# Bank-taking steps of the recurrent mixers issued in groups, and a planner estimate that charges for changes of operand form

## The chip, the cores and the metric

The kernel runs on one core of one Trainium2 chip. The metric is the device time of one execution in microseconds; three executions of the kernel before gave 1696.43, 1697.85 and 1698.03 us, median 1697.85.

## What is computed

Two layers of a hybrid encoder over 768 tokens (256 of a prompt, 512 of a sample; six tiles of 128 tokens). Each layer normalises, multiplies by one wide projection, runs three mixers side by side (windowed attention, a bidirectional mLSTM with 4 heads, a bidirectional Mamba-2 SSD with 8 heads), and merges them by gates and output projections:

```python
proj = rms_norm(x, norm_g) @ w_in
ya = window_attention(aq, ak, av, attn_sink) * silu(az)
yb = rms_norm(mlstm_bidir(mq, mk, mv, mi, mf)) * sigmoid(mo) * silu(mz)
yc = rms_norm(ssd_bidir(sx, sbm, scm, dt, a, d_skip) * silu(sz))
merged = ga * (ya @ w_att_out) + gb * (yb @ w_mlstm_out) + gc * (yc @ w_ssm_out)
return x + merged @ w_out
```

In the SSD each head needs, for each direction, a matrix of decays exp(acs_t - acs_s) under a causal mask; it is multiplied with C B^T and then with the head's inputs:

```python
lmat = exp(where(causal, acs[:, :, :, None] - acs[:, :, None, :], -inf))
y_diag = einsum('zclsg,zclsge,zcsgep->zclgep', cb, lmat, xdt)
```

## The kernel before, in words

**Products.** The large products (projection, gates, output projections) run on the TensorE in fp32r: every fp32 operand is split into a high and a low fp32r part, and three products are added. `mm_c` makes 128 output channels by all 768 tokens: for each of the three terms a matmul of 512 and one of 256 columns, here called a pair. A projection item has 24 pairs, an output product 12. `mm_t` makes a tile of 128 tokens by up to 512 channels. Weights come by DMA, are cast to the high part on ScalarE (`CAST R<-F`) and to the low part on VectorE (`TENSOR_TENSOR R<-F,R`), both in `split_w`. All small products of the mixers are plain fp32 (`psum<-F`): transposes, chunk states, scores and the products of the heads. So the TensorE changes between two forms of operand.

**The order of the work.** The whole program is written out in one pass by a planner; no engine reorders anything. The fp32r products form the backbone, in the order of the list `ORDER`. After every few matmuls `mm_c` and `mm_t` call `tick`, which lets waiting work go in between: tasks (`any_task`), weight splits (`split_next`) and mixers (`any_mixer`, two lanes). A mixer is a Python generator; it yields where it must wait, for a number of PSUM banks (`yield 1`, `yield 2`, `yield "pair"`), for an event, or for the time at which what it issued last is estimated to be done. `step` resumes it if `task.ready` has come by the planner's clock; where it wants banks, `grab` must find them free. The clock is an estimate: `Watched.cost` gives each instruction a length, and `Clock.note` adds it to the engine's time, behind what it depends on. `now` is the estimated time of the TensorE. `push` goes on without products where an item needs something that is not there yet.

**The mixers.** Lane 0 runs per layer: two attention groups (A0, A1), the four mLSTM heads (M), the SSD (S). `mix_ssd` first makes eight chunk states (`state`: GpSimd scales the inputs, two fp32 matmuls of 64 output rows, `64x256` in the order, then VectorE). Then six score products (`products`), then the heads (`head`, at most three at work). A head loads two broadcast rows of decays from HBM (`F<-csd`, 384 KB each, on SyncE's queue); for each direction VectorE subtracts and masks (six `SCALAR_TENSOR_TENSOR 128x128`), ScalarE takes the exponential (`ACTIVATE F<-F 128x768`) and, for the first direction, scales six times (`ACTIVATE 128x128`); VectorE adds the directions (six more) and multiplies with the scores (`TENSOR_TENSOR 128x768`); then come the head's six matmuls, `128x64`. Last, `across` adds what the chunk states give. `q_put` and `k_put` normalise and turn queries and keys at the start of a layer (GpSimd's power, then VectorE, for keys ScalarE, then transposes).

**Beside the heads** run the items `ob`: a gate product into PSUM, read by ScalarE (`ACTIVATE F<-psum 128x768`), an output product, read by VectorE (`SCALAR_TENSOR_TENSOR F<-F,psum`), an addition on GpSimd, and a store (`mg<-F`) on SyncE. Gate products take the two pairs of PSUM banks 0 to 3 in turn, so one waits for that reading ScalarE instruction.

Of the kernel before, what the change touches and what calls it, by code (L numbers as in the profile page):

```python
# [10 lines left out]
F32R = mybir.dt.float32r  # L11
# [15 lines left out]

RESERVE = 5000
AHEAD = 5
D = 1024  # L30
KD = 8
NT = 6
# [69 lines left out]
class Arena:  # L102
# [7 lines left out]
    def __init__(self, ap, words):  # L110
        self.ap, self.words = ap, words
        self.holes = [(0, words)]
# [200 lines left out]
class Watched:  # L313


    def __init__(self, engine, key, clock):
        self.engine, self.key, self.clock = engine, key, clock

    def __getattr__(self, name):
        fn = getattr(self.engine, name)  # L320
# [12 lines left out]
    def cost(self, name, out, ins, kw):  # L333
        n = 1
        for _, k in out.ap[1:]:
            n *= k
        key = self.key
        if key == "pe":
            if name == "transpose":
                return 107.0  # L340
            if ins[0].dtype == F32R:
                return 13.0 + n / 2.4

            if out.offset // out.ap[0][0] == 64:
                return 12.0
            return max(110.0 * 2, n / 0.6 + 6.0)
        if name == "dma_start":
            return 128 * n * 4 / 360.0
        if name == "tensor_reduce":
            n = 64 * n  # L350
        if key == "dve":
            three = name == "scalar_tensor_tensor" and all(a.tensor.name != self.clock.psum for a in ins)
            return 67.0 + n / 0.96 + (62.0 if three else 0.0)
        if key == "act":
            return 55.0 + 0.88 * n + (93.0 if "accum_out" in kw else 0.0)
        if kw.get("op") == ALU.pow:
            return 390.0 + 157.0 * n
        if name == "tensor_scalar":
            return 130.0 + 3.1 * n
        return 130.0 + 2.2 * n  # L360
# [47 lines left out]
class Body:  # L408
    def __init__(self, tc, es, ins, outs):
        self.tc = tc  # L410
        self.ins, self.outs = ins, outs
        self.clk = Clock()
        nc = self.nc = Watch(tc.nc, self.clk)
        sb = es.enter_context(tc.tile_pool(name="sb", bufs=1))
        ps = es.enter_context(tc.tile_pool(name="ps", bufs=1, space=bass.MemoryType.PSUM))
        dr = es.enter_context(tc.tile_pool(name="dr", bufs=1, space=bass.MemoryType.DRAM))
        RW, FW, WSLOT = 12288, 20096, 2048
        self.H = sb.tile([128, 2, KD, TOK], F32R, name="H")
        rt = sb.tile([128, RW + 4 * WSLOT], F32R, name="R")
        self.R = Arena(rt[:, 0:RW], RW)  # L420
        self.wslots = [rt[:, RW + WSLOT * j:RW + WSLOT * j + WSLOT] for j in range(4)]
        ft = sb.tile([128, FW], F32, name="F")
        self.F = Arena(ft, FW)
        self.psum = ps.tile([128, 8, 512], F32, name="psum")
        for t in (self.H[:, 0, 0, :], rt[:, 0:8], ft[:, 0:8]):
            self.clk.add(t)
        self.clk.add(self.psum[:, 0, :], True)
        self.held = [False] * 8
        self.x1 = dr.tile([TOK, D], F32, name="x1")
        self.mg = [dr.tile([8, 128, TOK], F32, name=f"mg{i}") for i in range(2 * NL)]  # L430
        self.tg = [dr.tile([8, 128, TOK], F32, name=f"tg{i}") for i in range(NL)]
        self.csd = [dr.tile([2, 48, 128], F32, name=f"csd{i}") for i in range(NL)]
        self.md = [dr.tile([2, 24, 128], F32, name=f"md{i}") for i in range(NL)]

        self.K = self.F.alloc(K_N).ap
        nc.sync.dma_start(out=self.K[:, K_ID:K_ID + 128], in_=ins["kst"][:, K_ID:K_ID + 128])
        self.ident = self.K[:, K_ID:K_ID + 128]
        self.masks = (self.K[:, K_MF:K_MF + 128], self.K[:, K_MB:K_MB + 128])
        self.expo = self.F.alloc(8).ap
        nc.vector.memset(self.expo, -0.5)  # L440
        self.raw_slots = [self.F.alloc(1024).ap for _ in range(2)]
        self.raw_extra = []
        self.cb = Ring(self.F, 1, CB_N)
        self.cc = Ring(self.F, 1, CC_N)
        self.zz = self.F.alloc(224).ap
        nc.vector.memset(self.zz, 0.0)
        self.ones = self.F.alloc(1).ap
        nc.vector.memset(self.ones, 1.0)

        self.pieces = []  # L450
        self.items = []
        self.wide, self.extra = set(), set()
        off = 0
        for l in range(NL):
            for kind, name, idx, pcs in item_plan(l):
                ids = []
                for p in pcs:
                    k, c = piece_shape(p)
                    ids.append(len(self.pieces))
                    self.pieces.append((off, k, c))  # L460
                    off += 128 * k * c
                self.items.append((l, kind, name, idx, ids))

                if kind == "W":
                    self.wide.update(ids)
                if name in ("akv", "sz"):
                    self.extra.update(ids)
        self.raw_of, self.w_of, self.w_task = {}, {}, {}
        self.n_raw = self.n_split = self.asked = 0
        self.raw_drop = []  # L470
        self.tasks = []
        self.done = {}
        self.lanes = [[], []]
        self.h_task, self.h_high = {}, [False] * NT
        self.S = [dict() for _ in range(NL)]


# [50 lines left out]
    def step(self, task, now):  # L528
# [11 lines left out]
        if isinstance(w, Room):  # L540
            if not w.there():
                return False
        elif isinstance(w, Task):
            if not w.over or w.ready > now:
                return False
        elif isinstance(w, tuple):
            if w not in self.done or self.done[w] > now:
                return False
        elif w is not None:
            got = self.grab(w, now)  # L550
            if got is None:
                return False
        kept, self.clk.last = self.clk.last, 0.0
        try:
            task.want = task.gen.send(got)
# [48 lines left out]

    def tick(self):

        while True:
            now = self.now
            if self.any_task(now) or self.split_next(now):
                continue  # L610
            if max(self.clk.free["dve"], self.clk.free["act"]) > now + BACKLOG or not self.any_mixer(now):
                return

    def push(self, until):

# [186 lines left out]
    def norm(self, x, g, i, sc, st):  # L802
# [3 lines left out]
        yield  # L806
        self.rstd(st[:, 1:2], st[:, 0:1], 1.0 / D)
        yield
# [19 lines left out]
    def layer0_start(self):  # L828
# [18 lines left out]
        for i in range(NT):  # L847
            self.h_task[i] = self.spawn(first(i, xr.next()))
            if i == 0:
                nc.sync.dma_start(out=gb.ap, in_=self.ins["ng"][0:1, :].to_broadcast([128, D]))  # L850
            if i < 2:
# [399 lines left out]
    def fetch(self, l, c):  # L1251

        s, nc = self.S[l], self.nc
        olds = s.setdefault("olds", {})
        for j in range(c, min(c + AHEAD, 8)):
            if j in olds:
# [664 lines left out]
```

## Time and profile before

| | us |
|---|---|
| median of three executions | 1697.85 |
| profiled execution, device time | 1698.3 |
| its span in the trace | 1696.5 |
| PE busy in the span | 1669.7 (98%) |
| DVE busy | 909.3 (54%) |
| ACT busy | 629.3 (37%) |
| POOL busy | 299.7 (18%) |
| granted TensorE clock, mean | 0.998 |

Times are counted from the start of the span. The TensorE is busy nearly throughout, so what counts is where it waits and how long its instructions hold it. Every instruction is recorded under one line (L323, a helper), so rows are told apart by engine, operands and shape. One fp32 matmul of the order stands in the trace as two records, unless it is a transpose. A row of the timeline merges instructions that follow each other on an engine: the start, the time they span, the count, and in brackets how long the engine sat idle before them and who ended that. The shape in a merged row is that of its first instruction. Ends of matmuls are modelled and reach some 0.2 us into the next row, so times of the TensorE are best read from start to start.

### The profile page before, as it was taken

What the parts mean: (1) busy time and instruction counts of PE and PEld (TensorE: products, weight loads), DVE (VectorE), ACT (ScalarE), POOL (GpSimd) and SP (SyncE); (2) the same over time, 40 slices, a digit from 0 to 9 for tenths busy, and PEclk for the clock granted to TensorE, in tenths of its full rate; (3) what the DMA queues carried; (4) which work ended last, traced back from release to release, by engine and by line L of the source; (5) the groups of instructions that cost most, each with busy time, mean ns of one, the idle gap of its engine ahead of it and who ended that gap; (6) DMA issues with size and microseconds to landing.
All of it is one profiled execution on the core that took longest, in us unless ns stands there. A gap on an engine that the chain in (4) does not pass through costs nothing.

```text
span 1696.5 us, 25376 instructions
## 1 busy us (share of the span) xinstructions
PE 1669.7 (98%) x9902; PEld 1435.2 (85%) x9902; DVE 909.3 (54%) x2112; ACT 629.3 (37%) x1377; POOL 299.7 (18%) x396
## 2 busy tenths in 40 slices
PE   7999999999999999999999999999999999999999
PEld 6888889888887888888878888898888878888887
DVE  6664446454485982246356544474455859723441
ACT  5446653232332532233224466442333344232320
POOL 4513210000002112014034132100000021301220
PEclk9999999999999999999999999999999999999999
DMA  5101122222213542245211101222121145331522
GB/s 203 63 27 38 51 76 78 87 69 64 68 63 114 190 147 91 72 144 175 78 44 63 52 26 50 88 88 78 69 72 60 63 140 174 134 109 44 174 87 75
DMA packets 47880, 152.17 MB, mean 90 GB/s; under 512 B 5616, under 2 KB 6544, under 8 KB 47760
## 3 DMA queue, kind: packets, MB, share of 16 engines
q1 hardware_dynamic: 47760, 150.55, 26.4%
q8 instruction: 78, 1.28, 0.3%
q14 instruction: 42, 0.34, 0.1%
HBM read 131.51 MB, written 19.02 MB: 89 GB/s over the span
## 4 chain that ended last, share of the span: by engine, by line
PE 87%; POOL 4%; DVE 3%; issue 3%; DMA 2%; ACT 1%; SPq 0%; POOLq 0%; ACTq 0%; DVEq 0%
PE psum L323 87%; POOL F L323 4%; DVE F L323 2%; DMA F<-csd 1%; DVE R L323 1%; DMA F<-wts_dram 1%; ACT F L323 0%; DMA F<-cstb_dram 0%; ACT R L323 0%; SPq L323 0%; ACT H L323 0%; DVE H L323 0%; POOLq L323 0%; ACTq L323 0%; DVEq L323 0%
## 5 line engine op out<-in xcount | busy, mean ns | idle before, releaser
L323 PE MATMUL psum<-H,R 128*128 128x512 f32 x4800 | 887.8, 341 | 0.0
L323 PEld LDWEIGHTS psum<-H,R 128*128 128x128 f32 x4800 | 734.1, 188 | 106.7 <-issue 6.5
L323 PE MATMUL psum<-R,H 128*128 128x512 f32 (+2 forms) x1752 | 386.2, 375 | 0.9 <-DVE F L323 0.5
L323 PEld LDWEIGHTS psum<-R,H 128*128 128x128 f32 x1752 | 306.1, 188 | 54.9 <-DVE R L323 1.4
L323 DVE TENSOR_TENSOR R<-F,R 128x1024 fp32r<-128x1024 f32 (+3 forms) x178 | 220.0, 1244 | 237.2 <-ACT R L323 235.2
L323 DVE SCALAR_TENSOR_TENSOR F<-F 128x128 f32<-128x128 f32 (+5 forms) x596 | 244.4, 456 | 76.8 <-POOL F L323 33.8
L323 POOL TENSOR_TENSOR F<-F 128x512 f32<-128x512 f32 (+9 forms) x216 | 203.3, 951 | 430.8 <-DVE F L323 255.0
L323 ACT ACTIVATE F<-F 128x128 f32<-128x128 f32 (+8 forms) x432 | 201.8, 496 | 207.2 <-DVE F L323 199.8
L323 PE MATMUL psum<-F 128*128 128x128 f32 (+5 forms) x2006 | 250.7, 288 | 22.6 <-DVE F L323 13.4
L323 PEld LDWEIGHTS psum<-F 128*128 128x128 f32 (+2 forms) x2006 | 203.0, 163 | 64.8 <-DVE F L323 22.0
L323 PE MATMUL psum<-R 128*128 128x512 f32 (+2 forms) x1344 | 250.1, 336 | 0.0
L323 ACT CAST R<-F 128x1024 fp32r<-128x1024 f32 (+3 forms) x226 | 195.1, 874 | 99.4 <-DVE F L323 58.3
L323 PEld LDWEIGHTS psum<-R 128*128 128x128 f32 x1344 | 204.4, 188 | 31.3 <-issue 3.6
L323 ACT ACTIVATE F<-psum 128x768 f32<-128x768 f32 (+2 forms) x124 | 89.0, 718 | 364.9 <-PE psum L323 329.9
L323 POOL TENSOR_SCALAR F<-F 128x256 f32<-128x256 f32 (+7 forms) x112 | 72.7, 652 | 755.0 <-ACT F L323 542.8
L323 ACT COPY F<-psum 128x256 f32<-128x256 f32 (+6 forms) x262 | 95.1, 400 | 176.6 <-PE psum L323 168.8
L323 DVE SCALAR_TENSOR_TENSOR F<-F,psum 128x768 f32<-128x768 f32 (+3 forms) x124 | 88.4, 725 | 102.8 <-ACT F L323 54.4
L323 DVE SCALAR_TENSOR_TENSOR F<-psum,F 128x128 f32<-128x128 f32 (+4 forms) x75 | 37.5, 505 | 172.8 <-PE psum L323 170.7
L323 DVE TENSOR_TENSOR F<-F 128x2 f32<-128x2 f32 (+8 forms) x316 | 86.3, 283 | 42.4 <-POOL F L323 22.7
L323 DVE TENSOR_SCALAR F<-F 128x128 f32<-128x128 f32 (+5 forms) x230 | 63.0, 302 | 41.0 <-ACT F L323 22.2
L323 DVE TENSOR_TENSOR F<-F,psum 128x129 f32<-128x129 f32 (+2 forms) x104 | 35.8, 376 | 36.4 <-ACT F L323 25.6
L323 DVE CUSTOM_DVE_ANT_0 F<-psum,F 128x256 f32<-128x256 f32 (+1 forms) x96 | 40.9, 464 | 10.4 <-PE psum L323 9.1
(24 smaller groups left out, 267.0 us busy)
## 6 DMA issues: line engine op xcount, KB each, us to landing
F<-wts_dram SPq DMA_DIRECT2D x164, 512.0 KB, 3.6
mg<-F SPq DMA_DIRECT2D x32, 384.0 KB, 2.9
F<-mg SPq DMA_DIRECT2D x32, 384.0 KB, 4.2
F<-csd SPq DMA_DIRECT2D x32, 384.0 KB, 7.0
F<-x_dram SPq DMA_DIRECT2D x12, 512.0 KB, 6.3
F<-md SPq DMA_DIRECT2D x16, 384.0 KB, 4.8
x<-F SPq DMA_DIRECT2D x6, 512.0 KB, 2.6
F<-x SPq DMA_DIRECT2D x6, 512.0 KB, 3.8
```

The lines of the kernel that those rows point to most:

```text
L323: r = fn(*args, **kw)
```

## The change

Two things are changed in the planner. No operand, tile or computation differs; only the order in which instructions stand does.

First, `Watched.cost` adds 50 ns to a TensorE instruction whose form (fp32r or not) differs from that of the one before.

Second, `tick` gets a gate. While the task at the head of lane 0 is an mLSTM head or the SSD (`calm`), steps that take PSUM banks may go in a tick only once the planner's clock has reached `gate`; a tick in which one went sets the gate 2000 ns ahead. Within an open tick any number may go. The gate holds for all tasks, not for lane 0 alone, and not in `push`.

```diff
+GROUP = 2000.0
...
         if key == "pe":
+            turn = 0.0 if self.split == (ins[0].dtype == F32R) else 50.0
+            self.split = ins[0].dtype == F32R
             if name == "transpose":
-                return 107.0
+                return 107.0 + turn
             if ins[0].dtype == F32R:
-                return 13.0 + n / 2.4
+                return 13.0 + n / 2.4 + turn
             if out.offset // out.ap[0][0] == 64:
                 return 12.0
-            return max(110.0 * 2, n / 0.6 + 6.0)
+            return max(110.0 * 2, n / 0.6 + 6.0) + turn
...
         elif w is not None:
+            if not self.open:
+                return False
             got = self.grab(w, now)
             if got is None:
                 return False
+            self.out = True
...
     def tick(self):
+        self.open, self.out = self.now >= self.gate or not self.calm(), False
         while True:
             now = self.now
             if self.any_task(now) or self.split_next(now):
                 continue
             if max(self.clk.free["dve"], self.clk.free["act"]) > now + BACKLOG or not self.any_mixer(now):
-                return
+                break
+        if self.out:
+            self.gate = self.now + GROUP
+        self.open = True
+
+    def calm(self):
+        return bool(self.lanes[0]) and self.lanes[0][0][0][1] in ("M", "S")
```

The order of the fp32r products is the same in both kernels; what stands between them moves. Stretches of fp32 matmuls on the TensorE go from 251 to 245; those of half-array matmuls (64 output rows, `64x...`) from 57 to 52.

**TensorE, the keys of layer 0.** The product of the last queries and the keys' projection (`128x288`); `F 128x128 x4` is the last query tile's transposes, each `F 128x128 x2` those of a key tile, in turn. Before:

```order
L323 MATMUL psum<-R,H 128x288 x60
L323 MATMUL psum<-F 128x128 x4
L323 MATMUL psum<-R,H 128x288 x6
L323 MATMUL psum<-F 128x128 x2
L323 MATMUL psum<-R,H 128x288 x18
L323 MATMUL psum<-F 128x128 x2
L323 MATMUL psum<-R,H 128x288 x24
```

and now:

```order
L325 MATMUL psum<-R,H 128x288 x54
L325 MATMUL psum<-F 128x128 x4
L325 MATMUL psum<-R,H 128x288 x30
L325 MATMUL psum<-F 128x128 x2
L325 MATMUL psum<-R,H 128x288 x12
L325 MATMUL psum<-F 128x128 x2
L325 MATMUL psum<-R,H 128x288 x12
```

The queries stand 6 products earlier, the first key tile 18 and the second 12 products later; the third stands where it did.

**SyncE's queue, the first heads of layer 0's SSD.** `F<-csd` are the heads' decays, `F<-mg` and `mg<-F` the load and store of an `ob` item, `F<-wts_dram` a piece of weights. Before:

```order
L323 DMA F<-wts_dram 128x1024
L323 DMA F<-mg_70 128x768
L323 DMA mg_71<-F 128x768
L323 DMA F<-csd_76 128x768 x6
L323 DMA F<-wts_dram 128x1024
```

and now:

```order
L325 DMA F<-wts_dram 128x1024
L325 DMA F<-mg_70 128x768
L325 DMA F<-csd_76 128x768 x6
L325 DMA mg_71<-F 128x768
L325 DMA F<-wts_dram 128x1024
```

The store has gone behind the six loads. The load of `mg` ahead of them now takes another buffer, and waits for the last of the score products.

**ScalarE, the same place.** From the copies of the score products on. `F<-F 128x768` is an exponential, `F<-F 128x128 x6` the scaling, `F<-psum` the reading of a gate product, `CAST` a weight split. Before:

```order
L323 COPY F<-psum 128x384 x4
L323 ACTIVATE F<-F 128x768
L323 ACTIVATE F<-F 128x128 x6
L323 ACTIVATE F<-psum 128x768
L323 CAST R<-F 128x1024
L323 ACTIVATE F<-F 128x768
L323 ACTIVATE F<-F 128x128 x6
L323 ACTIVATE F<-F 128x768
L323 CAST R<-F 128x1024
```

and now:

```order
L325 COPY F<-psum 128x384 x4
L325 ACTIVATE F<-F 128x768
L325 ACTIVATE F<-F 128x128 x6
L325 ACTIVATE F<-F 128x768
L325 ACTIVATE F<-F 128x128 x6
L325 ACTIVATE F<-psum 128x768
L325 CAST R<-F 128x1024
L325 ACTIVATE F<-F 128x768 x2
L325 CAST R<-F 128x1024
```

The exponential and the scalings of the second head have gone ahead of the reading of the gate product and of the cast. On the TensorE the score products stand 6 pairs earlier than before; the first three heads stand 14, 4 and 14 pairs earlier, the fourth 4, the other four as before. In layer 1 all of these stand at the same places.

## Rows read from the trace of the kernel before

**Rows 1.** TensorE's waits: total us, times, longest us.
```profile
PE psum L323 <- DVE F L323: 13.9, 12, 5.5
PE psum L323 <- ACT F L323: 6.2, 6, 1.2
```
**Rows 2.** Stages: us, busy by engine (count), clock, DMA share, GB/s; layer 0's mLSTM.
```profile
230.00:540.00 310.00, 310.00 (x1914) 271.59 (x1913) 176.21 (x397) 102.31 (x217) 21.30 (x27) 1.00 0.24 76
```
**Rows 3.** Timeline of TensorE, layer 0, the chunk states.
```profile
526.21 1.51 PE L323 MATMUL psum<-F 128*64 128x256 f32 x12
...
529.26 0.65 PE L323 MATMUL psum<-F 128*64 128x256 f32 x4
...
530.74 0.65 PE L323 MATMUL psum<-F 128*64 128x256 f32 x4
```
**Rows 4.** Timeline of TensorE, layer 0, score products and first three heads.
```profile
542.29 1.61 PE L323 MATMUL psum<-F 64*128 64x128 f32 x24
543.83 7.33 PE L323 MATMUL psum<-H,R 128*128 128x512 f32 x40
...
567.45 1.55 PE L323 MATMUL psum<-F 128*128 128x64 f32 x12 [1.45 <-DVE F L323]
...
570.02 1.55 PE L323 MATMUL psum<-F 128*128 128x64 f32 x12 [0.26 <-DVE F L323]
...
579.95 1.45 PE L323 MATMUL psum<-F 128*128 128x64 f32 x12
```
**Rows 5.** Timeline of SyncE's queue, the same place.
```profile
543.86 0.33 SPq L323 DMA_DIRECT2D mg<-F  x1
544.23 4.14 SPq L323 DMA_DIRECT2D F<-csd  x6
```
**Rows 6.** The chain that ended last, the third of these loads.
```profile
545.22 8.40 DMA F<-csd
```
**Rows 7.** Timeline of DVE, the same place.
```profile
549.30 1.66 DVE L323 SCALAR_TENSOR_TENSOR F<-F 128x128 f32<-128x128 f32 x6 [7.36 <-DMA F<-csd]
553.72 3.24 DVE L323 SCALAR_TENSOR_TENSOR F<-F 128x128 f32<-128x128 f32 x12 [2.75 <-DMA F<-csd]
556.88 1.21 DVE L323 TENSOR_TENSOR R<-F,R 128x1024 fp32r<-128x1024 f32 x1
...
561.16 0.94 DVE L323 SCALAR_TENSOR_TENSOR F<-F,psum 128x768 f32<-128x768 f32 x1
...
563.16 3.25 DVE L323 SCALAR_TENSOR_TENSOR F<-F 128x128 f32<-128x128 f32 x6
566.44 0.96 DVE L323 TENSOR_TENSOR F<-F 128x768 f32<-128x768 f32 x1
...
569.88 0.61 DVE L323 SCALAR_TENSOR_TENSOR F<-F,psum 128x384 f32<-128x384 f32 x1
```
**Rows 8.** Timeline of ACT, the same place.
```profile
551.00 2.74 ACT L323 ACTIVATE F<-F 128x768 f32<-128x768 f32 x7 [6.11 <-DVE F L323]
553.64 0.79 ACT L323 ACTIVATE F<-psum 128x768 f32<-128x768 f32 x1
554.34 1.03 ACT L323 CAST R<-F 128x1024 fp32r<-128x1024 f32 x1
```
**Rows 9.** Timeline of TensorE, layer 1, its first head.
```profile
1406.73 1.55 PE L323 MATMUL psum<-F 128*128 128x64 f32 x12 [1.25 <-DVE F L323]
```
**Rows 10.** Timeline of TensorE, key transposes: first and last of layer 0, fourth of layer 1.
```profile
68.91 0.44 PE L323 MATMUL psum<-F 128*128 128x128 f32 x2 [1.18 <-ACT F L323]
...
88.09 0.44 PE L323 MATMUL psum<-F 128*128 128x128 f32 x2 [0.99 <-ACT F L323]
...
917.52 0.44 PE L323 MATMUL psum<-F 128*128 128x128 f32 x2 [0.71 <-ACT F L323]
```
**Rows 11.** Timeline of TensorE, transposes in the first microseconds, after a wait.
```profile
15.03 1.97 PE L323 MATMUL psum<-F 128*128 128x128 f32 x8 [5.45 <-DVE F L323]
```
**Rows 12.** Stages, columns as in rows 2: around that wait.
```profile
11.20:18.00 6.80, 2.97 (x11) 2.77 (x12) 5.23 (x7) 4.67 (x8) 1.97 (x5) 0.50 0.94 369
```

More of the change, by code (lines that the diff above doesn't have):

```diff
@@ L317, in __init__ @@
         self.engine, self.key, self.clock = engine, key, clock
+        self.split = False
     def __getattr__(self, name):
@@ L474, in __init__ @@
         self.h_task, self.h_high = {}, [False] * NT
+        self.open, self.gate, self.out = True, 0.0, False
         self.S = [dict() for _ in range(NL)]
```

## The prediction

> **What bounds the kernel now.** First the busy times in the table: the TensorE (PE) works for 1669.7 of 1696.5 us, and since the change gives it the same instructions, only its waits, and what an instruction costs beside its neighbours, can move the time. So second the list of its waits: the two rows that matter are those for VectorE (12 waits) and ScalarE (6), 20.1 us together [rows 1]; 5.5 of it is one wait in the first microseconds, which the change doesn't touch. Third the stages: in the mLSTM of layer 0, where the gate acts most, the PE has no wait at all (310.00 busy of 310.00) [rows 2]. Fourth the timeline at each wait that is left: they lie at the norms, queries and keys at the start of a layer [rows 10], and before the first two heads of each layer's SSD [rows 4, 9]. At these the PE runs ahead of a chain of other engines. There the order decides, and I read what stands before and behind each wait in the orders shown above.
>
> **Fewer and longer stretches.** The orders have 251 stretches of fp32 work before and 245 after, so 12 changes of form fewer. No row prices one alone; 12 times the 0.05 us that the diff books is 0.6 us from above, zero from below; I take 0.1. More is saved where half-array matmuls join. One chunk state alone and two pairs of products fill 529.26 to 530.74, 1.48 us; three states joined and four pairs fill 526.21 to 529.26, 3.05 us [rows 3]. A pair costs (567.45 - 1.45 - 543.83) / 62 = 0.358 us (62 pairs lie between the score products and the first head) [rows 4]. So a state alone costs 0.76 us, three joined 1.62: each joining saves 0.33 us. Before, the states stand as 3, 1, 1, 1, 1, 1; now as 3, 2, 1, 2: two joinings, 0.66 us per layer. Attention has one stretch of half-array work fewer and `across` joins one more per layer; at 0.33 and half of that (not shown; zero to 0.33 each) another 0.6. Together 0.1 + 1.3 + 0.6 = 2.0 us gained, sure to within 0.8.
>
> **The first head of the SSD.** It now stands behind 54 pairs instead of 62, and the score products 6 pairs earlier. The PE's time first. Three states at 526.21; then 1.62, 6 pairs 2.15, two states 1.19 (midway between the two prices), 2.15, 0.76, 2.15, 1.19, 2.15: the score products start at 539.6 instead of 542.29 [rows 4] and end 1.54 later, at 541.1. After 54 pairs, 19.3 us, the PE would be at head 0 at 560.4. Before it was there at 566.0 and waited until 567.45 [rows 4].
>
> The data second. The six loads of decays were issued at 544.23, behind a store that had waited for GpSimd [rows 5]; this store now stands behind them, and a load that waits for the last score product stands ahead. So they go at 541.1 plus 0.55 for that load's issue (its like before took 0.33 to 0.55) = 541.65, 2.6 us earlier, not 5.6. Landing after issue as before: the first at 549.30 - 2.6 = 546.7 [rows 7], the third, which VectorE waits for next, 8.40 after its issue [rows 6]: 545.22 - 2.6 + 8.4 = 551.0. Sooner than the first's 5.1 us after issue it can't well be (547.8); an `mg` load and a piece of weights ahead could make it a microsecond later.
>
> From there ScalarE's new order counts. VectorE's six for the second head end at 552.7 (1.66 [rows 7]). ScalarE then takes the exponential and six scalings, 2.74, to 555.4, and only then reads the gate product, 0.79, and casts, 1.03 [rows 8]: 557.3. The weights' low part on VectorE waits for the cast: 1.21, 558.5. Behind it in order come six masks 1.66, the `ob` item's 0.94, the sum of the directions 3.25, the multiplication 0.96 [rows 7]: 565.3. So head 0 starts at 565.3 and the PE loses 4.9 us where it lost 1.45. Part of it comes earlier: the next gate product needs the bank that ScalarE reads until 556.2, and the PE is there after 39 pairs, at 555.0. That is 1.2 us of the 4.9, not more.
>
> **Heads 1 and 2.** Head 1 (12 pairs on, 4 earlier than before): VectorE needs a weight part 1.21, the first head's result 0.61 [rows 7] (from 566.9 on), 1.66 and 0.96: 570.1; the PE is there at 565.3 + 1.37 + 12 x 0.358 = 571.0. The 0.26 lost before [rows 4] goes. Head 2 (14 pairs on): masks 1.66, result 0.61 (from 572.5), weight part 1.21, sum 3.3, multiplication 0.96: 578.6; the PE is there at 571.0 + 1.37 + 5.0 = 577.4, and loses 1.2. Then level with before: 578.6 + 1.37 + 14 pairs 5.0 = 585.0, where before the head at 579.95 was done at 581.3 [rows 4]. So layer 0 loses 3.7 us here, the states' 0.66 and 2.77 us of moved work already in it. Bounds: with the third load at 547.8 the chain waits 2.1 less at best (ScalarE's scalings for the first head end at 551.2): 1.6 lost; with the loads 1 us later and head 3 late as well, 6. Layer 1 has the same orders at the same places, and its first head waits 1.25 [rows 9]: again 3.7. Sum 7.4, with the joining of states taken off.
>
> **Starts of the layers.** Here no gate holds; only the 50 ns move steps. Layer 0: the last queries go 6 products of 288 columns earlier, each 288 / 768 of a pair, 0.134 us; if their chain gives the time, 0.8 is lost, if not, nothing; I take 0.8. Keys 0 and 1 go 18 and 12 products later: their waits, 1.18 and nearly as much, go: 2.2 gained. The last key goes 2 pairs earlier onto a chain that is already late by 0.99 [rows 10]: 0.7 lost. Net 0.7 gained. Layer 1: the fourth key, 0.71 late already [rows 10], goes 6 products earlier, 0.8 lost, and the last 2 pairs earlier, 0.7 lost: 1.5. Both starts: 0.8 lost; -1 to +2.
>
> **The sum.** 7.4 + 0.8 - 0.7 (joinings outside the states) = 7.5; I round to 7.2, since a queue ahead of head 0 may hide some tenths. The mLSTM I cost at nothing: its steps now stand mostly 6 pairs, 2.1 us, apart, further from what they wait for, and the heads have no deadline near. Were that cover gone, a step's wait would be like those at the keys, 1 us. The profiled execution took 1698.3 us (span 1696.5), 0.45 above the median: 1698.3 + 7.2 = 1705.5, and beside the median 1705.0.
>
> **The clock.** After 5.45 us without work the PE's transposes took 1.97 us [rows 11], and from 11.20 to 18.00 the granted clock was 0.50, the lower of its two levels [rows 12]; it ran at full speed through waits of 1.5 us and less. From 15.03 to 18.00 at half speed costs 1.5 us. Head 0's wait of 3.7 us lies between. The Trainium skill (TensorE: Matmul & The Clock Gate, Part 1) says that an idle array falls to the lower clock and must work for a while before it gets the higher one back; that trace agrees. By that rule the two waits at head 0 would add up to 3.0 us.
>
> **The rivals.**
> A. The clock falls at head 0 of both layers, or head 3 waits too: 1705.0 + 3.0 = 1708. For it: the wait is over twice the longest that kept the clock. Against: part of it lies ahead, at the gate product, and a slower PE comes later to head 2, which takes back 1.2 per layer. Chance 0.2.
> B. No change. The chain to head 0 moves as far as the PE: the third load lands within 5.1 us, and the sum of directions takes 1.66, as where its instructions don't wait for each other, not 3.25. Then 1.6 less again per layer, so nothing is lost at the heads, and 1697.85 + 0.8 - 0.7 = 1698. Against: the loads of a burst landed one after another. Chance 0.15.
> C. Faster. The groups stand late enough: the heads' 1.7 and 1.5 us of waits go, the joinings give 2.0, keys 0 and 1 give 2.2: 1697.85 - 7.4 = 1690.5; with half the waits kept, 1693. For it: everywhere in the mLSTM and the states steps do stand later. Against: heads 0 and 2 stand earlier. Chance 0.12.
>
> **How the numbers follow.** My forecast has 0.53, at 1705.0, and its own range is 1701.5 to 1708.5. With B's upper and A's lower part, 8 in 10 lie in 1697 to 1710.5. A measurement of this kernel tells about 0.2%, 3.4 us, from no change. Slower by more: the forecast's 0.53 less 0.04, and A's 0.2, 0.69. Faster: C's 0.12. No change: 0.19.
>
> **What would show it.** Right: a wait for VectorE of some 4 us before each layer's first head, one of about 1 us for ScalarE at the gate product before it, the loads of decays issued 2 to 3 us earlier; two chunk states in about 1.2 us; waits gone at keys 0 and 1 of layer 0, grown at the last keys. Wrong: head 0 starting at once, loads issued before 541, a new wait in the mLSTM, or 1.66 us for the first sum of directions. The clock at 0.50 behind head 0 would show A.

## The result

The changed kernel takes 1712.84 us (median of four runs, 1712.34 to 1720.24); the kernel before, run beside it, 1697.94. The ratio is 1.010, with a 95% interval from 1.0083 to 1.0117: slower by 14.9 us. The forecast was 7.1 slower, its range ended at 1710.5. The side was right, the size was half.

TensorE's waits in the profile after (columns as in [rows 1]; the profiled execution took 1712.67 us, its span 1710.9):
```profile
PE psum L325 <- DVE F L325: 17.5, 14, 5.4
PE psum L325 <- ACT F L325: 11.8, 11, 2.4
...
PE psum L325 <- DVE R L325: 1.9, 2, 1.5
```
Against [rows 1], waits for VectorE grew by 3.6 us and those for ScalarE by 5.6; the last row was 0.4 before. That is 10.7 of the span's 14.4 us. The rest is no wait, as will be seen.

The place of the prediction, layer 0's SSD, on TensorE (columns of [rows 3, 4]):
```profile
529.47 1.52 PE L325 MATMUL psum<-F 128*64 128x256 f32 x12
...
542.78 1.61 PE L325 MATMUL psum<-F 64*128 64x128 f32 x24
...
560.38 7.38 PE L325 MATMUL psum<-H,R 128*128 128x512 f32 x32 [2.38 <-ACT F L325]
569.18 1.55 PE L325 MATMUL psum<-F 128*128 128x64 f32 x12 [1.42 <-DVE F L325]
570.54 4.59 PE L325 MATMUL psum<-H,R 128*128 128x512 f32 x16
...
576.36 1.45 PE L325 MATMUL psum<-F 128*128 128x64 f32 x12
...
582.64 1.45 PE L325 MATMUL psum<-F 128*128 128x64 f32 x12
...
595.35 8.59 PE L325 MATMUL psum<-H,R 128*128 128x512 f32 x48 [0.80 <-ACT F L325]
...
605.28 1.55 PE L325 MATMUL psum<-F 128*128 128x64 f32 x12 [0.66 <-DVE F L325]
```
The first states stood at 526.21 [rows 3]: 3.26 us are gone before the SSD begins. Then the gate product waits for ScalarE, head 0 for VectorE, heads 1 and 2 for nothing, and later a gate product and head 3 wait again. The row at 570.54 has 8 pairs in 4.59 us, without a wait in front.

Stages of the same trace around these waits (columns of [rows 2]):
```profile
560.60:564.00 3.40, 3.40 (x11) 2.89 (x11) 2.70 (x7) 3.08 (x4) 0.00 (x0) 0.51 0.14 30
564.00:569.10 5.10, 3.76 (x22) 3.06 (x20) 5.07 (x10) 2.72 (x7) 1.89 (x1) 1.00 0.44 163
570.80:574.20 3.40, 3.40 (x12) 2.82 (x12) 3.37 (x10) 0.00 (x0) 0.00 (x0) 0.50 0.85 211
```
The granted clock, third number from the end, was 0.50, the lower level, for 3.4 us right behind the gate product's wait, then full, then 0.50 again behind head 0's.

The other engines in the same microseconds (columns of [rows 5, 7, 8]). SyncE's queue, the loads of decays:
```profile
544.83 4.94 SPq L325 DMA_DIRECT2D F<-csd  x6
```
They are issued in one run, as in [rows 5], 0.6 us later by the clock and 2.7 earlier against the states. VectorE, from the first masks to head 0's multiplication:
```profile
551.74 1.67 DVE L325 SCALAR_TENSOR_TENSOR F<-F 128x128 f32<-128x128 f32 x6 [5.46 <-DMA F<-csd]
...
561.30 1.23 DVE L325 TENSOR_TENSOR R<-F,R 128x1024 fp32r<-128x1024 f32 x1 [1.61 <-ACT R L325]
...
564.01 0.95 DVE L325 SCALAR_TENSOR_TENSOR F<-F,psum 128x768 f32<-128x768 f32 x1
564.88 3.26 DVE L325 SCALAR_TENSOR_TENSOR F<-F 128x128 f32<-128x128 f32 x6
568.17 0.96 DVE L325 TENSOR_TENSOR F<-F 128x768 f32<-128x768 f32 x1
```
Its first load landed 6.9 us after the issue; the low part (561.30) waited for ScalarE. The third load, which the second head's masks wait for (columns of [rows 6]):
```profile
545.77 9.01 DMA F<-csd
```
ScalarE:
```profile
553.44 2.75 ACT L325 ACTIVATE F<-F 128x768 f32<-128x768 f32 x7 [8.07 <-DVE F L325]
556.90 2.74 ACT L325 ACTIVATE F<-F 128x768 f32<-128x768 f32 x7 [0.71 <-issue]
559.54 0.79 ACT L325 ACTIVATE F<-psum 128x768 f32<-128x768 f32 x1
560.23 1.03 ACT L325 CAST R<-F 128x1024 fp32r<-128x1024 f32 x1
```
The second row of seven is the second head's; it stood behind the gate product's read in [rows 8] and now stands ahead of it. GpSimd:
```profile
565.04 1.89 POOL L325 TENSOR_TENSOR F<-F 128x768 f32<-128x768 f32 x1 [16.84 <-DVE F L325]
```
VectorE's sum of directions (564.88) takes 3.26 us, as in [rows 7], and this addition lies inside it.

Outside the SSD the new waits stand in the attention of layer 0 and at the last keys of both layers:
```profile
87.64 0.44 PE L325 MATMUL psum<-F 128*128 128x128 f32 x2 [1.70 <-ACT F L325]
...
158.48 1.45 PE L325 MATMUL psum<-R,H 128*128 128x512 f32 x5 [1.49 <-DVE R L325]
...
936.97 0.44 PE L325 MATMUL psum<-F 128*128 128x128 f32 x2 [1.71 <-ACT F L325]
```
The first answers to the last key's 0.99 in [rows 10].

**Where the time went.** The fp32r products are the same stream in both kernels, so they serve as a ruler: for each TensorE instruction the time to the next one's start, less the usual time of its kind, summed between two places of the stream. Microseconds more than the kernel before, both layers together, from the profiled executions (the few tenths ahead of the first product are in the sum only):

| kernel | median | ratio, 95% | starts, attention | mLSTM | states | heads | behind the heads | sum |
|---|---|---|---|---|---|---|---|---|
| changed | 1712.84 | 1.0083–1.0117 | 4.98 | 0.30 | -1.14 | 13.30 | -2.96 | 14.42 |
| turn_only | 1701.73 | 1.0011–1.0030 | 5.89 | 1.57 | 0.02 | -2.98 | -1.04 | 3.26 |
| gate_only | 1707.46 | 1.0040–1.0065 | 0.24 | -0.66 | -1.13 | 10.07 | -1.16 | 7.27 |
| calm_turn | 1710.45 | 1.0045–1.0071 | 1.03 | -0.33 | -1.13 | 14.66 | -2.03 | 12.09 |
| act_first | 1707.55 | 1.0038–1.0074 | 5.36 | 0.30 | -1.14 | 7.13 | -0.43 | 11.06 |
| no_add | 1704.70 | 1.0025–1.0048 | 5.24 | 0.30 | -1.14 | 6.57 | -2.39 | 8.76 |
| gate_dma | 1697.87 | 0.9985–1.0004 | 1.19 | -0.66 | -1.13 | -4.71 | 5.01 | -0.38 |
| after_dma | 1698.17 | 0.9991–1.0009 | 5.39 | 0.30 | -1.14 | -1.92 | -2.11 | 1.03 |
| calm_late | 1694.40 | 0.9959–0.9982 | -0.28 | -0.33 | -1.13 | -2.16 | 0.29 | -3.83 |
| calm_late_slack | 1686.63 | 0.9910–0.9935 | -9.63 | -1.02 | -1.14 | -2.26 | 3.36 | -10.82 |
| before_slack | 1694.58 | 0.9963–0.9988 | -3.09 | -0.89 | 0.00 | -0.57 | 0.59 | -4.00 |
| best | 1689.47 | 0.9936–0.9961 | -3.38 | -1.67 | -1.14 | -1.86 | -0.60 | -8.75 |
| best_nogroups | 1695.54 | 0.9977–0.9995 | -3.62 | 0.10 | 0.01 | -3.32 | 4.18 | -2.73 |
| best2 | 1684.22 | 0.9903–0.9930 | -9.51 | -1.02 | -1.14 | -2.17 | -0.77 | -14.74 |

In a spell of the low clock a pair takes longer: the 16 products of 570.54 to 574.97 cost 1.57 us more than the same ones in gate_only, where the clock was full there; the first spell cost 1.56 against the same products in turn_only.

### The profile page after: what moved, and what is told of

Same layout as the page of the kernel before. It is cut to its first block, busy times and chain, and to the rows that moved or that the text cites. A ratio compares the mean times of both kernels' runs of the same rounds, so it can differ in the third digit from the quotient of the medians.

```text
span 1710.9 us, 25397 instructions
## 1 busy us (share of the span) xinstructions
PE 1673.4 (98%) x9902; PEld 1439.4 (84%) x9902; DVE 907.1 (53%) x2112; ACT 629.6 (37%) x1377; POOL 299.7 (18%) x396
## 4 chain that ended last, share of the span: by engine, by line
PE 87%; DVE 4%; DMA 3%; ACT 2%; issue 2%; POOL 2%; SPq 0%; ACTq 0%; DVEq 0%; POOLq 0%
PE psum L325 87%; DVE F L325 3%; DMA F<-csd 2%; POOL F L325 2%; ACT F L325 1%; DVE R L325 1%; DMA F<-wts_dram 1%; ACT R L325 0%; SPq L325 0%; DMA F<-cstb_dram 0%; ACT H L325 0%; DVE H L325 0%; POOL R L325 0%; ACTq L325 0%; DVEq L325 0%
```

## The experiments

**The two parts apart.** `turn_only` never closes the gate, `gate_only` books nothing.

```diff
     def calm(self):
...
-        return bool(self.lanes[0]) and self.lanes[0][0][0][1] in ("M", "S")
+        return False
```
```diff
-            turn = 0.0 if self.split == (ins[0].dtype == F32R) else 50.0
+            turn = 0.0 if self.split == (ins[0].dtype == F32R) else 0.0
```


> The change's 50 ns at every change of form alone; the groups never hold anything back. Theory (three losses: the bookings move the steps at the starts of the layers, the groups move the first heads of the SSD, and each longer wait drops the clock): the starts lose as in the changed kernel, 2.2 us more waits in layer 0 (with one in its attention) and about 2 in layer 1. In the SSD this order, too, has head 0 earlier, 58 pairs of products behind the score products (before 62, changed 54), with the loads of decays issued 1.7 us later against the products: a wait of 3 to 4 us at head 0 in one piece, none for ScalarE at the gate product (its read stands ahead of the second head's scalings again), and the clock at 0.50 behind it. Sum: 1698 + 4.2 + 2 x (2.2 + 1.0) = 1708.5. Rival 1 (the groups cause everything): 1698 within 1. Rival 2 (the bookings cause everything, heads included): 1713.

> The groups alone; a change of form books nothing. Up to head 2 of each SSD the order is that of the changed kernel. Theory: the starts wait as in the kernel before (L0's waits 12.8 us up to the states, not 15.0; no wait in the attention); the SSD loses as in the changed kernel, a wait of about 2.4 us for ScalarE at the gate product, 1.4 for VectorE at head 0 and the clock at 0.50 twice per layer, 6 us per layer; behind it the joined products give about 1 us back in layer 0 and 2 in layer 1. Sum: 1698 + 12 - 3 = 1707, with L0's states 0.4 to 0.7 earlier than before. Rival 1 (the groups cause everything): 1713. Rival 2 (the bookings cause everything): 1698 or up to 2 us less, heads without new waits.

The bookings alone lose 3.0 us (medians): by the table 5.9 at the starts and in the attention and 1.6 in the mLSTM, while the heads gain 3.0 and the stretch behind them 1.0. My 3 to 4 us at head 0 were wrong, it starts without a wait.
```profile
559.79 7.95 PE L325 MATMUL psum<-H,R 128*128 128x512 f32 x44
567.57 1.45 PE L325 MATMUL psum<-F 128*128 128x64 f32 x12
```
That is TensorE's timeline in turn_only; its loads were issued at 549.29, 18.3 us earlier, where the changed kernel needs 24.35 from issue to head. In turn_only the gate product is read ahead of the second head's scalings. The groups alone came as expected, 1707: starts as before, states 0.57 earlier per layer, heads late:
```profile
557.04 7.43 PE L325 MATMUL psum<-H,R 128*128 128x512 f32 x32 [1.79 <-ACT F L325]
565.84 1.55 PE L325 MATMUL psum<-F 128*128 128x64 f32 x12 [1.38 <-DVE F L325]
567.20 3.02 PE L325 MATMUL psum<-H,R 128*128 128x512 f32 x16
```
Behind head 0 of layer 0 the clock held this time (last row, against 4.59 in the changed kernel). I had expected two spells of the low clock per layer, and there is one: in layer 0 behind the gate product, in layer 1 behind head 0, which waits 2.96 us there (the gate product 1.18, with no spell). So each part has its own loss, and neither rival (all groups, all bookings) stands. The two losses, 3.0 and 8.7, do not make up the changed kernel's 14.9. By the table the difference lies at the heads: 13.30 in the changed kernel against 10.07 and -2.98. turn_only's gain (its head 0 stands 58 pairs behind the score products) is not there, and 3.2 us come on top, of which 1.57 are layer 0's second spell and 0.59 its longer wait at the gate product (2.38 against 1.79).

**Bookings kept from the starts.** `calm_turn` is the changed kernel with the 50 ns booked only while the gate may act.
```diff
-            turn = 0.0 if self.split == (ins[0].dtype == F32R) else 50.0
+            turn = 0.0 if self.split == (ins[0].dtype == F32R) or not self.clock.calm else 50.0
...
+        self.clk.calm = self.calm()
```


> The changed kernel, but the 50 ns are booked only while the mixers of a layer work at the mLSTM or the SSD, not at the starts of the layers; states, score products and heads stand as in the changed kernel. Theory (the 50 ns cost 5 us at the starts and in layer 0's attention, and the rest of the loss is the SSD's): the starts wait as in the kernel before, the SSD with its spells stays: 1712.8 - 4.9 = 1708. Rival (the loss moves: whatever is saved at the starts is lost at the next wait): 1712.

The starts come back to within 1.0 us of the kernel before, so the bookings cause their loss. The span fell by only 2.2 us (1708.7 against 1710.9), since the heads lost 1.4 more: the gate product's wait (2.04) brought no spell, TensorE was at head 0 sooner and waited 2.87 us there, and one spell of 6.8 us followed, so in both layers. The rival has a part in this: the order at the heads is the changed kernel's, the loss is not.
```profile
567.08 2.82 PE L326 MATMUL psum<-F 128*128 128x64 f32 x12 [2.87 <-DVE F L326]
```

**The price of the clock.** `filler` gives TensorE products to do in the two waits of each layer.
```diff
+FILL_AT, FILL = (973312, 2554880), 10
...
+            if self.key == "pe" and name == "matmul" and kw["rhs"].dtype == F32R:
+                if self.cols in FILL_AT:
+                    self.clock.body.fill(FILL)
+                self.cols += kw["out"].ap[-1][1]
...
+    def fill(self, n):
+        b = min((b for b in range(4, 8) if not self.held[b]), key=lambda b: self.clk.bank[b])
+        for _ in range(n):
+            self.tc.nc.tensor.matmul(out=self.psum[:, b, :], lhsT=self.H[:, 0, 0, 0:128], rhs=self.H[:, 0, 0, 0:512], start=True, stop=True)
...
+            if h == 0:
+                self.fill(FILL)
```
`FILL_AT` counts the columns of the fp32r products up to the waiting gate product of each layer.


> The changed kernel; TensorE (PE) runs 10 more 128x512 products (about 2.2 us), whose results nobody reads, where it waits at the gate product and again where it waits at head 0, in both layers; all else keeps its order. In the changed kernel the clock fell to 0.50 for 3.41 us behind each of these four waits, and each such spell cost the products 1.56 us more than their usual pace. Theory (the spell behind the gate product lies in front of a head that waits for VectorE anyway, so only the spell behind head 0 costs time): the spells go, head 0 starts when it did, 2 x 1.56 = 3.1 us are gained: 1709 to 1710.5. Rival 1 (every spell costs its 1.56): 1712.8 - 6.2 = 1706.6. Rival 2 (the spells are hidden behind later waits anyway): 1712 to 1714.

Measured 1710.23 (ratio 1.0047 to 1.0074), and no spell is left in either SSD. TensorE in layer 0, and VectorE's multiplication for head 0:
```profile
558.21 2.49 PE L515 MATMUL psum<-H 128*128 128x512 f32 x10
560.54 5.80 PE L331 MATMUL psum<-H,R 128*128 128x512 f32 x32
566.18 2.46 PE L515 MATMUL psum<-H 128*128 128x512 f32 x10
568.66 1.55 PE L331 MATMUL psum<-F 128*128 128x64 f32 x12
570.02 3.02 PE L331 MATMUL psum<-H,R 128*128 128x512 f32 x16
```
```profile
567.65 0.96 DVE L331 TENSOR_TENSOR F<-F 128x768 f32<-128x768 f32 x1
```
At full clock the 16 pairs behind the gate product take 5.80 us instead of 7.38, but head 0 starts only as its data are there, 568.6. Counted from the score products that is 0.9 us sooner than in the changed kernel, as much as the third load landed sooner in this execution; in layer 1 it is 0.2 later. So the first spell lies ahead of a head that waits for its data, and costs nothing. The second is lost in full, 4.59 less 3.02. Against the changed kernel 2.4 us are gained by the spans, and 3.9 by the medians when each is taken less that of its own kernel before; the theory said 3.1, rival 1 6.2, rival 2 none.

**Why the gate product waits.** `act_first` holds the second head's first exponential back, so that ScalarE reads the gate product first.
```diff
+            if h == 0:
+                self.done["late", l] = self.now + 9000.0
...
-                yield
+                yield ("late", l) if (h, d) == (1, 0) else None
                 sc.activation(out=L[d], in_=L[d], func=AF.Exp, scale=-1.0)
```


> The changed kernel; the second head's first exponential and its six scalings are held back 9 us by the planner's clock, so that ScalarE reads the gate product ahead of them. The planner then puts head 0 earlier, 46 pairs behind the score products (changed: 54); loads and score products stand where they stood. Theory (the wait at the gate product is ScalarE's order, and head 0 waits for its own place): no wait at the gate product (2.38 us in the changed kernel); the cast, VectorE's low part of the weights and head 0's data come about 2.6 us earlier against the score products, and TensorE, there 8 pairs (2.9 us) earlier, waits 5 to 6 us at head 0 in one piece. Rival (the gate product is late because the first load lands late, whatever the order): it still waits 2 us or more.

The wait at the gate product is gone; the products run through to head 0:
```profile
558.18 2.99 PE L325 MATMUL psum<-H,R 128*128 128x512 f32 x16
562.82 1.55 PE L325 MATMUL psum<-F 128*128 128x64 f32 x12 [1.64 <-DVE F L325]
```
So it was ScalarE's order. But head 0 waited only 1.64 us where I expected 5 to 6. On VectorE its sum of directions now follows the weights' low part at once:
```profile
560.11 1.66 DVE L325 SCALAR_TENSOR_TENSOR F<-F 128x128 f32<-128x128 f32 x6
```
Six masks (1.66 us) and the `ob` item's product (0.95), which stand ahead of the sum in the changed kernel, stand behind it here, which I had not counted. That is 2.6 us. The rest is the sum itself, 1.66 us instead of 3.26, with the addition on GpSimd behind it, at 563.71. What makes the sum slow is what the next run asks. (act_first has two executions only, 1705.67 and 1709.43.)

**What makes the sum slow.** In this run GpSimd's addition is left out, and the planner books it as if it were there.
```diff
-                nc.gpsimd.tensor_tensor(out=th.ap, in0=th.ap, in1=old.ap, op=ALU.add)
+                g = nc.gpsimd
+                g.clock.note("pool", g.cost("tensor_tensor", th.ap, [th.ap, old.ap], {"op": ALU.add}), [th.ap], [th.ap, old.ap])
```


> The changed kernel; GpSimd's additions of the mLSTM's part to the attention's part (one 128x768 addition per ob item, just behind VectorE's product of that item) are left out, with the planner booking them as before, so that the order stays; that part of the sum is missing from the output. In every trace so far the one slow instruction in a head's sum of directions (1.94 us for one of 128x128 where its five neighbours take 0.34) began within 1.3 us of such an addition and ended with it. Theory (VectorE's sum and GpSimd's addition stop each other, and this is 1.6 us of each head's chain): the sums take 1.66 instead of 3.26 us, the waits for VectorE at heads 0 and 3 (1.42 and 0.94 us in layer 0) go, and with the first of them the second spell of the low clock, 1.56: 3 to 4 us per layer, 1705 to 1707; the wait for ScalarE at the gate product (2.38) stays, with its spell. Rival (the sum waits for ScalarE's scalings): sums stay at 3.26, 1712.

Measured 1704.70, 8.1 us less than the changed kernel by the medians, 5.7 by the spans. VectorE and TensorE in no_add:
```profile
564.23 0.95 DVE L325 SCALAR_TENSOR_TENSOR F<-F,psum 128x768 f32<-128x768 f32 x1
565.09 1.66 DVE L325 SCALAR_TENSOR_TENSOR F<-F 128x128 f32<-128x128 f32 x6
566.78 0.96 DVE L325 TENSOR_TENSOR F<-F 128x768 f32<-128x768 f32 x1
```
```profile
560.59 7.38 PE L325 MATMUL psum<-H,R 128*128 128x512 f32 x32 [2.02 <-ACT F L325]
567.81 1.54 PE L325 MATMUL psum<-F 128*128 128x64 f32 x12
569.16 3.02 PE L325 MATMUL psum<-H,R 128*128 128x512 f32 x16
```
The sum takes 1.66. In layer 0 head 0 does not wait and the second spell is gone, while the gate product's wait and its spell stay, as the theory says. In layer 1 the sum takes 1.66 as well, but the clock goes another way:
```profile
1403.07 5.82 PE L325 MATMUL psum<-H,R 128*128 128x512 f32 x32 [1.26 <-ACT F L325]
1410.28 1.91 PE L325 MATMUL psum<-F 128*128 128x64 f32 x12 [1.39 <-DVE F L325]
```
The gate product's wait is shorter there (1.86 in the changed kernel) and no spell follows, so TensorE is at head 0 sooner, waits 1.39 us, and the one spell of that layer stands behind head 0. The theory's part on the sum holds in both layers, its part on the second spell in layer 0 alone.

**Heads asked for later.** `gate_dma`, `after_dma` and `calm_late` are gate_only, the changed kernel and calm_turn with one more edit:
```diff
-            fin = self.free["dma"] + 900.0
+            fin = self.free["dma"] + (5000.0 if any(x.tensor.name.startswith("csd") for x in ins) else 900.0)
```


> The groups alone, and the planner books 5.0 us instead of 0.9 behind a load of decays (its landing), so that it asks for the heads later: head 0 stands 64 pairs of products behind the score products (changed 54, before 62), and ScalarE reads the gate product ahead of the heads' scalings. Theory (the SSD loses because the heads are asked for before their decays can be there): the waits at gate product and head 0 go, the clock stays at 1.0, and the joined states and products stay: 1698 - 3 (waits of both SSDs before) - 3 (joinings) = 1692 to 1695. Rival (the groups themselves delay the heads' chain, whatever the place): waits of 1 us or more at the heads still, 1700 or more.

> The changed kernel with the 5.0 us behind a load of decays; the 50 ns stay. Head 0 stands as in the run with groups alone and these 5.0 us. Theory: the SSD as there, the starts as in the changed kernel: 4.2 us more than that run, so 1696 to 1699. Rival (the 50 ns hurt in the SSD and not in the starts): within 1 us of that run.

> As calm_turn, and the planner books 5.0 us instead of 0.9 behind a load of decays, so that head 0 stands 64 pairs behind the score products and the last head has 3 more places than with the groups alone. Theory: the starts of the kernel before with the SSD of after_dma (states 0.57 and SSD 1.0 better per layer, 2.1 behind the SSDs): 1698.7 - 5.2 = 1693 to 1694.5. Rival (the starts take it back): 1698.

In all three the heads' waits go and they end 1.9 to 4.7 us better than before: the loss at the heads was one of place, not of the groups. after_dma and calm_late came as expected, 1698.17 and 1694.40, 3.8 us apart, by the bookings at the starts. gate_dma missed (1697.87): its last two heads are pushed to the end of the SSD, and the last waits:
```profile
630.63 1.45 PE L325 MATMUL psum<-F 128*128 128x64 f32 x12
633.85 2.03 PE L325 MATMUL psum<-F 128*128 128x64 f32 x12 [1.77 <-DVE F L325]
```
A spell of the low clock follows it; 5.0 us are lost behind the heads. Late heads need room at the end as well.

**The starts.** These three are calm_late with steps held 0.8 us longer. `calm_late_slack` holds every step outside mLSTM and SSD; `best` leaves out the end of layer 0, and with it the steps ahead of layer 0's first projections; `best2` has these again (its edit is shown; best lacks the first two lines in `start`).
```diff
-        task.ready = max(task.ready, self.clk.last + Clock.HOP)
+        task.ready = max(task.ready, self.clk.last + Clock.HOP + (800.0 if self.start() else 0.0))
...
+    def start(self):
+        if not self.lanes[0]:
+            return self.layer == 0
+        return self.lanes[0][0][0][0] == self.layer and self.lanes[0][0][0][1] in ("A0", "A1")
```


> As calm_late, and at the starts of the layers (where neither mLSTM nor SSD is at work) every step is held 0.8 us longer after what it needs, by the planner's clock. The waits at the starts were 5.6 us in layer 0 and 7.4 us in layer 1 before, each 0.6 to 1.4 us. Theory (there the planner books the chains of the norms, queries and keys too short by about a microsecond): half to all of the shorter waits go: 4 to 8 us less than calm_late, 1686 to 1690. Rival (the steps are on a chain that ends late wherever they stand, since each held step holds the next): as calm_late or slower, 1694 to 1700.

> As calm_late_slack, but the 0.8 us hold only from a layer's first projections to the end of its attention, not at the end of layer 0, where calm_late_slack had a new wait of 2.37 us for VectorE in the norm and a spell of the low clock behind it. Theory: that wait and the spell go, about 3 us less: 1683 to 1685. Rival (the end of layer 0 waits for a chain that was already late): 1686 to 1688.

> As best, with the 0.8 us also ahead of layer 0's first projections, where best lost 2.80 us of waits (64.6 and 66.8 us from the start), a spell of the low clock and 1.43 us in the attention, which calm_late_slack didn't. Theory (the steps of the first norm must be held as well, or the order at the start of layer 0 turns worse): layer 0's start and attention as in calm_late_slack, 6 us less than best, and the end of layer 0 as in best: 1682.5 to 1684.5. Rival (the end of layer 0 gains its 3.7 us only where the start was late): 1686 to 1687.

calm_late_slack takes 1686.63, as expected; its new wait is at the end of layer 0:
```profile
803.25 1.09 PE L326 MATMUL psum<-F 128*128 128x128 f32 x8 [2.37 <-DVE F L326]
```
best gained 4.0 us there against calm_late_slack, but lost 6.2 at the starts and in the attention (1689.47, a miss). best2 has both, 1684.22, expected 1682.5 to 1684.5: 0.8% faster than the kernel before (ratio 0.9903 to 0.9930), the fastest of all. Its waits:
```profile
PE psum L326 <- DVE F L326: 9.9, 9, 5.4
...
PE psum L326 <- ACT F L326: 0.2, 1, 0.2
```
Two runs show what of this is the change's. `before_slack` has the same held steps (as in best) in the kernel before; `best_nogroups` is best with a gate that never closes:
```diff
-            if not self.open:
+            if False:
                 return False
```

> The kernel before, with the 0.8 us at the starts of the layers alone (no groups, no 50 ns, 0.9 us behind a load of decays). Theory (the waits at the starts come from chains that the planner books too short, with the change or without): 4.5 to 5 us less in each layer's start, the rest as in the kernel before: 1699 - 10 = 1689. Rival (the gain needs the groups): 1696 or more.

> As best, but the groups hold nothing back; the 50 ns in mLSTM and SSD, the 5.0 us behind the loads of decays and the 0.8 us at the starts stay. Theory (the groups by themselves are worth the joined states, 0.57 us per layer, and up to 1 us of joined products behind each SSD): 1 to 3 us more than best, 1685 to 1687. Rival (the groups cost time even where the heads come late enough): 1 us or more below best.

before_slack takes 1694.58, not 1689: layer 1's start gives back 5.4 us, about as expected, but layer 0's fails as in best. The rival (it needs the groups, 1696 or more) falls. best_nogroups is 6.1 us slower than best, against 1 to 3 expected: 1.15 from states, 1.8 in the mLSTM, 4.8 behind the heads, less 1.5 at the heads. In that order the groups are worth more than the joinings alone; why, behind the heads, was not followed further than a wait and a spell of 6.8 us there.

## Why the prediction was half right

**First head of the SSD: right, and well placed.** Counted from the first state, the score products were forecast at 13.4 us and came at 13.31; head 0 at 39.1 and came at 39.71; head 2 at 52.4 and came at 53.17. The loads went out behind the `mg` load, ScalarE read the gate product behind the second head's scalings, and the gate product waited, all as written. Its wait was 2.38 us, not 1.2: the third load landed 9.0 us after its issue (8.40 taken), the second head's exponential began some 0.4 us behind its masks (nothing taken), and TensorE was there 0.3 sooner. act_first shows the cause given, ScalarE's order. The wait at head 0 itself was 1.42 us where 3.7 were left for it, since the longer wait and the first spell (1.56) came out of the same time. That head 2 came near its forecast is luck, as the next paragraph shows.

**The step that failed: "Then level with before ... So layer 0 loses 3.7 us here", and "Sum 7.4".** States and heads lost 6.2 and 5.9, together 12.2. My sum ended at head 2; behind it the next gate product and head 3 wait 0.80 and 0.66 us, which I had only as a bound ("head 3 late as well"). And the 1.2 us that I gave to a wait of head 2 was no wait: filler and no_add have none there. In its place stood the second spell of the low clock, 1.57 us per layer, which my sum did not have.

**The clock: rival A came in part.** It had the fall at head 0; it did not have that the gate product's wait alone brings one, nor that it costs nothing there. At its two places the rival said up to 3.0 us, and filler gave 2.4 to 3.9. By the Trainium skill (TensorE: Matmul & The Clock Gate, Part 1) an array that falls idle drops to the lower clock and must earn the higher one back. These rows agree: 0.50 for 3.4 us behind the waits, with TensorE busy all the time (3.40 of 3.40 us), then 1.00.

**The sum of directions: taken at its length, without its cause.** I costed 3.25 us from [rows 7] and held 1.66 for possible if "its instructions don't wait for each other". They wait for GpSimd, as no_add shows, and the addition is released by the `ob` item that stands right ahead of the sum. Without that pairing head 0 of layer 0 would have had no wait, and no second spell behind it.

**Starts and attention: the other miss.** Forecast 0.8 lost, measured 4.98. The starts alone lost 0.28 in layer 0 and 2.44 in layer 1 (forecast -0.7 and 1.5): in layer 0 the waits at keys 0 and 1 went, as written, but the last queries wait 1.62 us (0.8 taken) and a later key 0.69. For the attention the sum had only the gain of a joined stretch; any loss there was put at nothing without a reason, and layer 0's lost 2.59, of which the new wait for VectorE is 1.49. The gate has no part in this: turn_only loses as much, gate_only and calm_turn do not. I had followed the transposes of queries and keys through the order and not the attention's.

**States and joinings: right, a little high.** Per layer 0.57 us instead of 0.66; behind the heads more came back than the 0.7 I had, 2.96. The mLSTM, costed at nothing, lost 0.30.

## What to carry to other kernels

Where a planner writes the order, a change of its costs or rules is judged by the chains that it moves the main engine towards: count on to where both orders are level again, past the last place that the difference touches. A wait of the TensorE has two prices, its own and that of the spell of half clock behind it, and the second costs only what no later wait absorbs. Steps that are asked for before their data can be there are cured by booking what the trace shows: with 5 us behind a broadcast load, 0.8 us at the chains of the starts and the 50 ns booked in mLSTM and SSD alone, the same groups ended 13.8 us ahead of the kernel before (1684.22 against 1698.06). Not all of this is theirs: the kernel before gained 4.2 us from 0.8 us at its starts (before_slack).

## What the runs showed of the hardware

**VectorE and GpSimd stop each other.** Six instructions of 128x128 with two operands in SBUF take 1.66 us. Where GpSimd's addition of 128x768 falls on them, one of the six takes 1.94 us instead of 0.34 and all 3.26; where VectorE was already at work on a weight's low part, the addition itself takes 2.76 us instead of 1.84 to 1.89. In the changed kernel 8 of 480 such VectorE instructions take 1.93 to 2.02 us, each ending 0.15 us behind an addition; in no_add none does. GpSimd in the kernel before, the first row inside the time of [rows 7]:
```profile
562.18 2.76 POOL L323 TENSOR_TENSOR F<-F 128x768 f32<-128x768 f32 x1 [18.36 <-DVE F L323]
574.74 1.84 POOL L323 TENSOR_TENSOR F<-F 128x768 f32<-128x768 f32 x1 [9.79 <-DVE F L323]
```
No list of waits names this, since the stopped instruction counts as busy. The Trainium skill (SBUF — State Buffer, SBUF: two separate sides) says that the two engines share a pair of ports as an exclusive lock, held for a whole instruction, against VectorE's operations with two inputs in SBUF. The runs agree: 1.94 us instead of 0.34 on one side, 2.76 instead of 1.84 on the other.

**Short waits can halve the clock.** Spells of 3.4 us at 0.50 followed waits of 2.38, 2.37, 1.79 and 1.77 us, one of 1.64 in act_first and one of 1.42 (head 0 of the changed kernel); a spell of 6.8 us followed one of 1.27 in best_nogroups. None followed the 1.70 and 1.71 at the last keys, the 1.38 at the same head 0 in gate_only, or 2.04 at the gate product of calm_turn. So the length of a wait alone does not tell; what else does, these runs leave open.
